# Down-projection of an 8-chunk FFN group: gating at the exit from PSUM, accumulation into DRAM by DMA, and another order for an inner tile's differences

## The chip, the cores and the metric

The kernel runs on one core of one Trainium2 chip. The metric is device time in microseconds (us); 3 runs of the kernel before took 1652.31 to 1652.87, with a median of 1652.55. The core has engines that run side by side, each with its own queue in order: TensorE (PE) multiplies matrices into PSUM, VectorE (DVE) and ScalarE (ACT) do elementwise work and can read PSUM, GpSimd (POOL) and SyncE (SP) issue DMAs here. A wait in a queue holds everything behind it.

## The reference

One step of a diffusion backbone, one trunk layer, for 128 context and 512 latent tokens of width 1024, in float32:

```python
h = modulate(rmsnorm(x, norm_g[0]), sh1, sc1)
x = x + 0.5 * g1 * swiglu(h, ffn1_w1, ffn1_w2)
h = modulate(rmsnorm(x, norm_g[1]), shm, scm)
y, C, n, m = mixer(h, ...)          # mLSTM both ways, short convolution
x = x + gm * y
h = modulate(rmsnorm(x, norm_g[2]), sh2, sc2)
x = x + 0.5 * g2 * swiglu(h, ffn2_w1, ffn2_w2)
```

where `swiglu(h, w1, w2) = (silu(a) * b) @ w2` and a, b are the halves of `h @ w1`, with an inner width of 2816 = 22 chunks of 128. A final RMSNorm follows. The gate g2 is one vector for context tokens and another for latent tokens. Only the second feed-forward network (FFN) is touched by the change.

## The kernel before, in words

Activations lie transposed: X is 8 tiles of 128 channels by 640 tokens (T), split in halves of 320 (HT): the first half has all 128 context tokens and 192 latent ones, so its gate needs two column ranges, 0 to 128 and 128 to 320; the second half needs one. To keep float32 accuracy, each operand is split into a high part (a cast, ScalarE, line 75) and a low part (a subtraction, VectorE, line 79), and each product is three matmuls (`three`, lines 245 to 247).

Two blocks of weights are multiplied together as a **pair** by a Strassen-like scheme (`pair_steps`): seven products instead of eight, in the order A11, S1, S2, A12, S3, S4, A22, each twelve matmuls of 128x320. Their weights are quarter blocks or sums of them (ws, line 218, VectorE). Their activations are eight lists of four tiles: 11, 21, 22 and the differences T1 to T4; A11 takes 11, S1 takes T1, S2 takes T2, A12 takes 21, S3 takes T3, S4 takes 22, A22 takes T4. Four accumulators in PSUM (a, b, e, c) pass through: b starts as ScalarE's copy of a (line 280), c as its copy of b (line 290); S1's result is copied out as p5 (line 286); after S3, c is read to make c22 = c + p5 (line 301 on VectorE, or with `spare_v` line 298 on ScalarE and 299 on VectorE); only then may A22 go on writing c. After S4, b + p5 (line 304) is handed out. `ev(mi, h, src)` takes the result for block mi and token half h. The results of block 1 are handed out late, at the A11 step of the next pair (`flush`).

At each product the kernel first emits the weight preparation for the product four places ahead (sum, cast, low part), then the matmuls, then what reads the result. After product number i the list `at[i]` is called: work put there by hand. `lazy` is a list of postponed steps, of which `relax` calls all and `relax_some(n)` n. So the order in which each engine's queue gets its work is the order of these calls; no planner changes it.

The second FFN runs in groups of 8, 8 and 6 chunks. A group of eight (`eights`) has two phases. First come the **gate pairs** j: block a and block b of chunk j; ScalarE takes silu of a (line 1033), VectorE multiplies by b (line 1035), giving sa for both token halves. In chunks 0 to 3 that makes list 11 and T1 (steps `left`, `diff1`); in chunks 4 to 7 the steps `diff2`, `diff3`, `diff4` finish T2, 21, 22 and the raw values of T3 and T4 (`raw3`, `raw2`, lines 1019, 1024, 1028), which lie in X's SBUF tiles since X has been stored to DRAM (`xd`, by `spill_x`). In the first group, chunks 0 and 1 are made by an element ahead of the pairs, which leaves a stock of six postponed steps. Then come four **down pairs** m = 0, 2, 4, 6: two blocks of w2 by the eight lists, whose results are gated and added to X. For that X tiles are loaded from DRAM (`x_back`), updated by `add_x` (line 953: x = ps * gate + x on VectorE, three instructions per block), and stored (`x_away`). T3 and T4 of the network's input, saved in `hd`, are loaded again in the last down pair (`h_back`): eight loads after S3, eight after A22. All these DMAs stand in POOL's queue. The gate's columns are `modT[:, g, m, 0:1]` for latent and `1:2` for context tokens. The six-chunk group at the end uses other code and X in SBUF; `x_whole` loads it.

Of the kernel before, what the change touches and what calls it, by code (L numbers as in the profile page):

```python
# [44 lines left out]
def mixer_step(ctx: ExitStack, tc: tile.TileContext, x_prompt, x_sample, state_C, state_n, state_m,  # L45
# [23 lines left out]
    def t3():  # L69
        return tp.tile([P, HT], F32, name="t3", bufs=8)  # L70
# [171 lines left out]
    def three(ps, hi, lo, kk, act, start, stop):  # L242
        ws = slice(kk * P, (kk + 1) * P)
        ah, al = act
        PE.matmul(ps, hi[:, ws], ah, start=start, stop=False, skip_group_check=True)  # L245
        PE.matmul(ps, hi[:, ws], al, start=False, stop=False, skip_group_check=True)  # L246
        PE.matmul(ps, lo[:, ws], ah, start=False, stop=stop, skip_group_check=True)  # L247
# [15 lines left out]
    def relax_some(n):  # L263
        for _ in range(min(n, len(lazy))):
            lazy.pop(0)()

    def pair_steps(order, ev, spare_v, acts):
        S = {}

        def prod(name, ps, start):  # L270
            hi, lo = op()
            for kk in range(4):
                three(ps[:, :HT], hi, lo, kk, acts[ACT_OF[name]][kk], start and kk == 0, kk == 3)

        for name in order:
            if name == "A11":
                S["a"] = big()
                prod(name, S["a"], True)
                S["b"] = big()
                A.copy(S["b"][:, :HT], S["a"][:, :HT])  # L280
                flush()
            elif name == "S1":
                e = big()
                prod(name, e, True)
                S["p5"] = t3()
                A.copy(S["p5"], e[:, :HT])
            elif name == "S2":
                prod(name, S["b"], False)
                S["c"] = big()
                A.copy(S["c"][:, :HT], S["b"][:, :HT])  # L290
            elif name == "A12":
                prod(name, S["a"], False)
                ev(0, 0, S["a"][:, :HT])
            elif name == "S3":
                prod(name, S["c"], False)
                S["c22"] = t3()
                if spare_v:
                    A.copy(S["c22"], S["c"][:, :HT])
                    V.tensor_add(S["c22"], S["c22"], S["p5"])
                else:  # L300
                    V.tensor_add(S["c22"], S["c"][:, :HT], S["p5"])  # L301
            elif name == "S4":
                prod(name, S["b"], False)
                V.tensor_add(S["p5"], S["b"][:, :HT], S["p5"])
                ev(0, 1, S["p5"])
            else:
                prod(name, S["c"], False)
                late.append(lambda: ev(1, 0, S["c"][:, :HT]))
                late.append(lambda: ev(1, 1, S["c22"]))
            yield  # L310

    def pair_el(load1, load2, ev, e1=None, spare_v=False, acts=HB, at=None, calm=False):
        po = pair_ops(e1=e1)
        at = at or {}

        def emit():
            nf = len(fill)
            for i, _ in enumerate(pair_steps(ORDER, ev, spare_v, acts)):
                if not calm:
                    relax(7 - i if i else 9)  # L320
                drain(nf - nf * (i + 1) // 7)
                for f in at.get(i, ()):
                    f()
        return dict(element([load1, load2], [po[name] for name in ORDER], emit), pair=True)
# [637 lines left out]
            SQ.pop(0)()  # L962


    def x_back(m, x):
        G.dma_start(x, xd[m])

    def x_away(m, x):
        G.dma_start(xd[m], x)

    def h_away(*names):
        for o in names:
# [4 lines left out]
    def h_back(o):  # L977
        for k in range(4):
            HB[o][k] = hpair(o)
            for i in range(2):  # L980
                G.dma_start(HB[o][k][i], hd[o, k, i])

    def eights(w1, w2, g, f0, n_head, head, more, back):

        spare = (n_head, n_head + 1, 7) if f0 < n_head else (7,)
        UB = {o: [None] * 4 for o in OPS_H}

        def tile_of(m):
            if "xs" not in PO:
                PO["xs"] = [xp.tile([P, T], (F32, F32R)[i // 4], name="x", bufs=KT) for i in range(KT)]  # L990
            return PO["xs"][m]
        slot = lambda a, k: tile_of(2 * a + k // 2)[:, hsl(k % 2)]
        raw3 = lambda k: slot(0, k)
        raw2 = lambda k: slot(1, k)

        def put_own(o, k, src):
            UB[o][k] = hl = upair()
            split(src, *hl)

        def put_22(k, src):  # L1000
            UB["22"][k] = hl = [tile_of(4 + k)[:, hsl(i)] for i in range(2)]
            split(src, *hl)

        def put_lent(o, k, src):
            UB[o][k] = hl = hpair(o)
            split(src, *hl)

        def ev_of(j):
            sa, k = {}, j % 4

            def left():
                put_own("11", k, sa[0])

            def diff1():
                V.tensor_sub(raw2(k), raw3(k), sa[0])
                put_own("T1", k, raw2(k))

            def diff2():
                V.tensor_sub(raw2(k), sa[1], raw2(k))
                put_own("T2", k, raw2(k))  # L1020

            def diff3():
                put_own("21", k, sa[0])
                V.tensor_sub(raw3(k), sa[1], raw3(k))

            def diff4():
                put_22(k, sa[1])
                V.tensor_sub(raw2(k), sa[0], raw2(k))

            def ev(mi, h, src):  # L1030
                if mi == 0:
                    sa[h] = raw3(k) if h and j < 4 else t3()
                    A.activation(sa[h], src, AF.Silu)
                    return
                V.tensor_mul(sa[h], src, sa[h])
                if h == 0:
                    if j < 4:
                        lazy.append(left)
                else:
                    lazy.extend([diff1] if j < 4 else [diff2, diff3, diff4])  # L1040
            return ev
        grp = []
        for j in range(8):
            p = (w_load(w1, 0, KT, (f0 + j) * P, 2 * DFF), w_load(w1, 0, KT, DFF + (f0 + j) * P, 2 * DFF), ev_of(j))
            at = {}
            if j == 7:
                lent = lambda k: lambda: put_lent("T3", k, raw3(k))
                at = {4: [lent(0), lent(1), lent(2)], 6: [flush]}
            due = j - n_head if f0 < n_head else 8
            if due:  # L1050
                at[1] = [relax if due > 2 else lambda n=due + 2: relax_some(n)]
            if f0 + j < n_head:
                head.extend(blocks_of(p))
            else:
                grp.append(pair_el(*p, at=joined(at, more.get(j, {})), spare_v=j in spare, calm=True))
        w2s = []
        away = lambda *ms: [lambda m=m: x_away(m, tile_of(m % 4)) for m in ms]
        come = lambda *ms: [lambda m=m: x_back(m, tile_of(m % 4)) for m in ms]
        PO["x_end"] = away(6, 7)
        for m in range(0, KT, 2):  # L1060
            ev = lambda mi, h, src, m=m: add_x(m + mi, h, src, g, False, tile_of((m + mi) % 4))
            at = {}
            if m == 0:
                four = lambda k: lambda: put_lent("T4", k, raw2(k))
                at = {0: [relax], 1: [lambda: put_lent("T3", 3, raw3(3))] + come(0, 1) + [four(0)],
                      2: [four(1)], 3: [four(2), four(3)] + come(2, 3)}
            else:
                at = {1: away(m - 2, m - 1)}
                if m + 2 < KT:
                    at[2] = come(m + 2, m + 3)  # L1070
                else:
                    at[4] = [lambda: h_back("T3")] if back else []
                    at[6] = [lambda: h_back("T4")] if back else []
            w2s.append(pair_el(w_load(w2, f0 * P, 8, m * P, D), w_load(w2, f0 * P, 8, (m + 1) * P, D), ev,
                               spare_v=True, acts=UB, at=at))
        return grp, w2s

    def ffn(w1, w2, g, lists, head_of, n_head, e1=None, groups=(6, 6, 6, 4), more={}):
# [1051 lines left out]
    def x_whole():  # L2130
        for m in range(KT):
            x_in(m)
    x_end = [lambda: [f() for f in PO["x_end"]]]
    x_in_last = {1: x_end, 2: [x_whole]}
    more = {0: {3: {0: [lambda: h_away("T3", "T4")]}},
            1: {0: {1: x_end}}, 2: {0: x_in_last}}
    head, els = ffn(ffn2_w1, ffn2_w2, G2, y_after, lambda bl: head_el(bl, *right_chain(2, SH2), mod_mid(G2, 0)), 2,
                    groups=(8, 8, 6), more=more)
    els[0][0][0]["fill"] = [step(f) for f in N["later"] + [lambda: None] * 6]
# [37 lines left out]
```

## Time and profile before

| | |
|---|---|
| runs, median (range) | 1652.55 us (1652.31 to 1652.87) |
| profiled execution | 1651.78 us, its span 1649.9 us |
| granted TensorE clock | 0.999 |
| busy: PE, PEld (weight loads), DVE, ACT, POOL | 1628.9, 1585.9, 1319.5, 826.4, 223.3 us |
| first group: gate pairs, down pairs | about 1240 to 1319, 1319 to 1368 us |
| second group: gate pairs, down pairs | about 1368 to 1467, 1467 to 1518 us |
| X tiles: loads and stores of 320 KB from POOL | 32 and 32, 4.0 and 5.4 us from issue to landing |

A timeline row has the start in us from the span's start, the duration, the engine, the line, the operation, output and inputs with their shapes, and in brackets the idle time just ahead and what ended it. A row of a group has the count, the total in us and the mean in ns. A row of windows has the stretch, its length, and the busy time with the number of instructions for PE, PEld, DVE, ACT and POOL, then the clock, the DMA share and GB/s. Matmuls overlap each other: they start about 0.15 us apart and take 0.31.

### The profile page before, as it was taken

How to read it: one execution, taken by the hardware profiler on the slowest of the kernel's cores; microseconds unless marked ns; L12 is line 12 of the kernel's file. 1: busy time of each engine (PE TensorE's matmuls, PEld its weight loads, DVE VectorE, ACT ScalarE, POOL GpSimd, SP SyncE). 2: the span in 40 equal slices, each digit the busy share in tenths (PEclk: the TensorE clock that was granted, in tenths of full speed). 3: DMA queues.
4: the chain of work that ended last, by engine and by line, in shares of the span. 5: the costliest groups of instructions: out<-in, count | busy, mean ns of one | idle time of the engine just before them, and what ended most of it. 6: DMA issues, size and time to landing. Idle time of an engine off the chain costs nothing.

```text
span 1649.9 us, 29478 instructions
## 1 busy us (share of the span) xinstructions
PE 1628.9 (99%) x11093; PEld 1585.9 (96%) x11093; DVE 1319.5 (80%) x2786; ACT 826.4 (50%) x1805; POOL 223.3 (14%) x354
## 2 busy tenths in 40 slices
PE   8999999999999999999999999999999999999998
PEld 5999999999999999999999999999999999999997
DVE  6867887887778878788897899779688897898765
ACT  5642542542566655465561455633275555564443
POOL 2010000000031321221121221011112012003002
PEclk9999999999999999999999999999999999999999
DMA  9454343343353433342258432357355256337522
GB/s 321 116 165 120 105 128 112 103 125 94 114 172 102 102 101 90 84 118 71 84 180 263 113 90 78 106 169 222 117 166 141 84 178 175 88 117 219 172 81 64
DMA packets 283661, 216.68 MB, mean 131 GB/s; under 512 B 9331, under 2 KB 260602, under 8 KB 283520
## 3 DMA queue, kind: packets, MB, share of 16 engines
q1 hardware_dynamic: 263152, 158.36, 33.4%
q0 software_dynamic: 20336, 56.45, 11.5%
q8 instruction: 87, 1.43, 0.4%
q14 instruction: 54, 0.44, 0.1%
q10 hardware_dynamic: 32, 0.01, 0.0%
HBM read 188.98 MB, written 25.79 MB: 130 GB/s over the span
## 4 chain that ended last, share of the span: by engine, by line
PE 89%; DVE 4%; ACT 3%; DMA 2%; issue 1%; POOL 0%; SPq 0%; ACTq 0%; DVEq 0%
PE ps L245 27%; PE ps L246 27%; PE ps L247 27%; PE ax L1717 2%; PE ax L1748 2%; PE ax L1720 1%; DVE wl L79 1%; ACT wh L75 1%; ACT Uh L867 1%; DMA early<-in_w_mod_dram 1%; DMA HT4l<-hd 1%; PE ax L1694 1%; DMA wr<-in_ffn_w_dram 0%; ACT Uh L75 0%; DVE Uh L859 0%
## 5 line engine op out<-in xcount | busy, mean ns | idle before, releaser
L79 DVE TENSOR_TENSOR wl<-wr,wh 128x512 fp32r<-128x512 f32 (+1 forms) x389 | 261.4, 684 | 79.8 <-ACT wh L75 77.5
L75 ACT CAST wh<-wr 128x512 fp32r<-128x512 f32 (+1 forms) x391 | 230.2, 600 | 89.1 <-PE ps L246 69.3
L79 DVE TENSOR_TENSOR wl<-ws,wh 128x512 fp32r<-128x512 f32 x324 | 228.0, 704 | 39.5 <-ACT wh L75 38.7
L75 ACT CAST wh<-ws 128x512 fp32r<-128x512 f32 x324 | 199.0, 620 | 108.9 <-DVE ws L218 71.4
L245 PE MATMUL ps<-Uh,wh 128*128 128x320 f32 x576 | 179.8, 312 | 0.0
L246 PE MATMUL ps<-Ul,wh 128*128 128x320 f32 x576 | 177.9, 309 | 0.2
L247 PE MATMUL ps<-Uh,wl 128*128 128x320 f32 x576 | 177.7, 309 | 0.0
L245 PE MATMUL ps<-HT4h,wh 128*128 128x320 f32 x408 | 128.5, 315 | 0.2 <-DVE t L301 0.2
L246 PE MATMUL ps<-HT4l,wh 128*128 128x320 f32 x408 | 126.3, 309 | 0.5 <-DMA HT4l<-hd 0.4
L247 PE MATMUL ps<-HT4h,wl 128*128 128x320 f32 x408 | 126.0, 309 | 0.0
L245 PE MATMUL ps<-H11h,wh 128*128 128x320 f32 x376 | 118.8, 316 | 0.7 <-ACT H11h L75 0.7
L245 PE MATMUL ps<-H21h,wh 128*128 128x320 f32 x376 | 117.7, 313 | 0.0
L246 PE MATMUL ps<-H11l,wh 128*128 128x320 f32 x376 | 116.5, 310 | 0.3
L247 PE MATMUL ps<-H21h,wl 128*128 128x320 f32 x376 | 116.2, 309 | 0.0
L247 PE MATMUL ps<-H11h,wl 128*128 128x320 f32 x376 | 116.1, 309 | 0.0
L246 PE MATMUL ps<-H21l,wh 128*128 128x320 f32 x376 | 116.0, 308 | 0.0
L245 PE MATMUL ps<-HT3h,wh 128*128 128x320 f32 x356 | 112.0, 315 | 3.5 <-ACT ps L290 3.5
L246 PE MATMUL ps<-HT3l,wh 128*128 128x320 f32 x356 | 110.0, 309 | 0.0
L247 PE MATMUL ps<-HT3h,wl 128*128 128x320 f32 x356 | 110.0, 309 | 0.0
L245 PEld LDWEIGHTS ps<-Uh,wh 128*128 128x128 f32 x576 | 108.1, 188 | 1.4 <-issue 0.8
L246 PEld LDWEIGHTS ps<-Ul,wh 128*128 128x128 f32 x576 | 108.1, 188 | 0.7 <-DVE Ul L79 0.7
L247 PEld LDWEIGHTS ps<-Uh,wl 128*128 128x128 f32 x576 | 108.1, 188 | 0.0
(477 smaller groups left out, 4699.4 us busy)
## 6 DMA issues: line engine op xcount, KB each, us to landing
wr<-in_ffn_w_dram SPq DMA_DIRECT2D x102, 512.0 KB, 3.9
wr<-in_w_in_dram SPq DMA_DIRECT2D x72, 512.0 KB, 3.9
wr<-in_w_mod_dram SPq DMA_DIRECT2D x51, 512.0 KB, 3.9
wr<-in_ffn_w_dram SPq DMA_DIRECT2D x32, 384.0 KB, 3.3
xd<-x POOLq DMA_DIRECT2D x32, 320.0 KB, 5.4
x<-xd POOLq DMA_DIRECT2D x32, 320.0 KB, 4.0
early<-in_w_mod_dram SPq DMA_DIRECT2D x13, 512.0 KB, 9.0
mg<-in_w_mod_dram POOLq DMA_DIRECT2D x8, 512.0 KB, 5.6
```

The costliest lines, as they stand in the source:

```text
L75: A.copy(hi, raw)
L79: V.tensor_sub(lo, raw, f32(hi))
L245: PE.matmul(ps, hi[:, ws], ah, start=start, stop=False, skip_group_check=True)
L246: PE.matmul(ps, hi[:, ws], al, start=False, stop=False, skip_group_check=True)
L247: PE.matmul(ps, lo[:, ws], ah, start=False, stop=stop, skip_group_check=True)
L867: A.activation(t[:, a:b], t[:, a:b], AF.Identity, scale=sc_, bias=bi_)
L1694: PE.matmul(p[:, :P], S["k", dt][:, sl], S["q", dt][:, sl], start=(dt == 0), stop=(dt == 1))
L1717: PE.matmul(p2[:, :DH + 1], S["q", dt][:, sl], S["C"][d][:, dt, :], start=(dt == 0), stop=(dt == 1))
L1720: PE.matmul(p1[:, :DH + 1], S["p", ch][:, d, :], PO["vt"][:, ch, :], start=True, stop=True)
L1748: PE.matmul(p[:, :DH + 1], kw[:, dt * P:(dt + 1) * P], PO["vt"][:, ch, :], start=True, stop=True)
```

## The change

In the groups of eight, X no longer comes back for the down pairs. A result is gated on its way out of PSUM into a free SBUF tile y, and a DMA with accumulation adds y to X in DRAM.

- S1's result is taken out twice by ScalarE, multiplied by the latent gate of block 0 and of block 1 (the second token half has latent tokens only).
- After S3 and after S4, one VectorE instruction makes gate * accumulator + gated p5 straight from PSUM, into the second half of y. This replaces lines 298, 299 and 304 there.
- The first half of y is made by two ScalarE activations (Copy with the gate as scale), for 128 and 192 tokens.
- `x_add` issues one accumulating DMA per block from POOL; `x_back` and `x_away` are gone, and `x_end` with them.
- `x_whole` (the six-chunk group) moves from its gate pair 0 to pair 2.
- The steps of an inner tile are reordered: list 21 is now made in `diff2`, 22 in `diff3`, and T2 with the last subtraction in `diff4`. In the gate pairs two postponed steps are called after S1, and after A12 two more (first group, pairs 3 and 4) or all the rest; before, all were called after S1 (three and four in pairs 3 and 4).

```diff
-    def pair_steps(order, ev, spare_v, acts):
+    def pair_steps(order, ev, spare_v, acts, gated=None):
...
+        def gated_sum(i, ps):
+            y, g = gated(i)
+            V.scalar_tensor_tensor(y[:, HT:], ps[:, :HT], g, S["p5"][i], op0=OP.mult, op1=OP.add)
...
-                S["p5"] = t3()
-                A.copy(S["p5"], e[:, :HT])
+                if gated:
+                    S["p5"] = [t3(), t3()]
+                    for i in range(2):
+                        A.activation(S["p5"][i], e[:, :HT], AF.Copy, scale=gated(i)[1])
...
+                if gated:
+                    gated_sum(1, S["c"])
...
+                if gated:
+                    gated_sum(0, S["b"])
+                    ev(0, 1, None)
...
-    def x_back(m, x):
-        G.dma_start(x, xd[m])
-
-    def x_away(m, x):
-        G.dma_start(xd[m], x)
+    def x_add(m, y):
+        G.dma_start(xd[m], y, accum_op=OP.add)
...
             def diff2():
                 V.tensor_sub(raw2(k), sa[1], raw2(k))
+                put_own("21", k, sa[0])
+
+            def diff3():
+                V.tensor_sub(raw3(k), sa[1], raw3(k))
+                put_22(k, sa[1])
+
+            def diff4():
                 put_own("T2", k, raw2(k))
-
-            def diff3():
-                put_own("21", k, sa[0])
-                V.tensor_sub(raw3(k), sa[1], raw3(k))
-
-            def diff4():
-                put_22(k, sa[1])
                 V.tensor_sub(raw2(k), sa[0], raw2(k))
...
-                at[1] = [relax if due > 2 else lambda n=due + 2: relax_some(n)]
+                at = joined(at, {1: [lambda: relax_some(2)], 3: [lambda: relax_some(2)] if due < 3 else [relax]})
...
+            rows_ = lambda i, m=m: (tile_of((m + i) % 4), modT[:, g, m + i, 0:1])
+
+            def ev(mi, h, src, m=m):
+                y = tile_of((m + mi) % 4)
+                if h:
+                    x_add(m + mi, y)
+                    return
+                for a, b, cd in ((0, P, 1), (P, HT, 0)):
+                    A.activation(y[:, a:b], src[:, a:b], AF.Copy, scale=modT[:, g, m + mi, cd:cd + 1])
...
-    more = {0: {3: {0: [lambda: h_away("T3", "T4")]}},
-            1: {0: {1: x_end}}, 2: {0: x_in_last}}
+    more = {0: {3: {0: [lambda: h_away("T3", "T4")]}}, 2: {2: {1: [x_whole]}}}
```

More of the change, by code (lines that the diff above doesn't have):

```diff
@@ L284, in pair_steps @@
                 prod(name, e, True)
-                S["p5"] = t3()
-                A.copy(S["p5"], e[:, :HT])
+                if gated:
+                    S["p5"] = [t3(), t3()]
+                    for i in range(2):
+                        A.activation(S["p5"][i], e[:, :HT], AF.Copy, scale=gated(i)[1])
+                else:
+                    S["p5"] = t3()
+                    A.copy(S["p5"], e[:, :HT])
             elif name == "S2":
@@ L295, in pair_steps @@
                 prod(name, S["c"], False)
-                S["c22"] = t3()
-                if spare_v:
+                S["c22"] = None if gated else t3()
+                if gated:
+                    gated_sum(1, S["c"])
+                elif spare_v:
                     A.copy(S["c22"], S["c"][:, :HT])
@@ L303, in pair_steps @@
                 prod(name, S["b"], False)
-                V.tensor_add(S["p5"], S["b"][:, :HT], S["p5"])
-                ev(0, 1, S["p5"])
+                if gated:
+                    gated_sum(0, S["b"])
+                    ev(0, 1, None)
+                else:
+                    V.tensor_add(S["p5"], S["b"][:, :HT], S["p5"])
+                    ev(0, 1, S["p5"])
             else:
@@ L310, in pair_steps, with pair_el @@
             yield
-    def pair_el(load1, load2, ev, e1=None, spare_v=False, acts=HB, at=None, calm=False):
+    def pair_el(load1, load2, ev, e1=None, spare_v=False, acts=HB, at=None, calm=False, gated=None):
         po = pair_ops(e1=e1)
@@ L317, in emit @@
             nf = len(fill)
-            for i, _ in enumerate(pair_steps(ORDER, ev, spare_v, acts)):
+            for i, _ in enumerate(pair_steps(ORDER, ev, spare_v, acts, gated)):
                 if not calm:
@@ L1056, in eights @@
         w2s = []
-        away = lambda *ms: [lambda m=m: x_away(m, tile_of(m % 4)) for m in ms]
-        come = lambda *ms: [lambda m=m: x_back(m, tile_of(m % 4)) for m in ms]
-        PO["x_end"] = away(6, 7)
         for m in range(0, KT, 2):
-            ev = lambda mi, h, src, m=m: add_x(m + mi, h, src, g, False, tile_of((m + mi) % 4))
+            rows_ = lambda i, m=m: (tile_of((m + i) % 4), modT[:, g, m + i, 0:1])
[6 more added lines that the diff above has]
+                    A.activation(y[:, a:b], src[:, a:b], AF.Copy, scale=modT[:, g, m + mi, cd:cd + 1])
             at = {}
@@ L1064, in eights @@
                 four = lambda k: lambda: put_lent("T4", k, raw2(k))
[L1065 to L1073, printed above, removed]
+                at = {0: [relax], 1: [lambda: put_lent("T3", 3, raw3(3)), four(0)], 2: [four(1)], 3: [four(2), four(3)]}
+            elif m == KT - 2 and back:
+                at = {4: [lambda: h_back("T3")], 6: [lambda: h_back("T4")]}
             w2s.append(pair_el(w_load(w2, f0 * P, 8, m * P, D), w_load(w2, f0 * P, 8, (m + 1) * P, D), ev,
-                               spare_v=True, acts=UB, at=at))
+                               acts=UB, at=at, gated=rows_))
         return grp, w2s
@@ L2132, in x_whole @@
             x_in(m)
-    x_end = [lambda: [f() for f in PO["x_end"]]]
-    x_in_last = {1: x_end, 2: [x_whole]}
-    more = {0: {3: {0: [lambda: h_away("T3", "T4")]}},
-            1: {0: {1: x_end}}, 2: {0: x_in_last}}
+    more = {0: {3: {0: [lambda: h_away("T3", "T4")]}}, 2: {2: {1: [x_whole]}}}
     head, els = ffn(ffn2_w1, ffn2_w2, G2, y_after, lambda bl: head_el(bl, *right_chain(2, SH2), mod_mid(G2, 0)), 2,
```

## The prediction

> **What bounds the kernel now.** I read the page first, then the waits of TensorE, then the timeline around each place where TensorE paused.
>
> ```profile
> span 1649.9 us, 29478 instructions
> PE 1628.9 (99%) x11093; PEld 1585.9 (96%) x11093; DVE 1319.5 (80%) x2786; ACT 826.4 (50%) x1805; POOL 223.3 (14%) x354
> ...
> PE ps L245 <- ACT ps L290: 3.5, 4, 2.2
> ...
> PE ps L246 <- DMA HT4l<-hd: 0.4, 1, 0.4
> ...
> PE ps L245 <- DVE t L301: 0.2, 1, 0.2
> ```
>
> TensorE is busy 99% of the span and the change leaves its 11093 matmuls alone. So time can come only from pauses of TensorE, and in the stages that change there are few: waits for ScalarE's copy at L290, one for a DMA, one for VectorE. The timeline of TensorE gives each (a bracket is the idle time that it shows).
>
> ```profile
> 1285.70 0.31 PE L247 MATMUL ps<-H21h,wl 128*128 128x320 f32 x1
> 1288.24 0.41 PE L245 MATMUL ps<-HT3h,wh 128*128 128x320 f32 x1 [2.22 <-ACT ps L290]
> 1288.49 0.31 PE L246 MATMUL ps<-HT3l,wh 128*128 128x320 f32 x1
> ...
> 1273.42 0.42 PE L245 MATMUL ps<-HT3h,wh 128*128 128x320 f32 x1 [0.75 <-ACT ps L290]
> 1292.22 0.41 PE L245 MATMUL ps<-HT4h,wh 128*128 128x320 f32 x1 [0.20 <-DVE t L301]
> 1326.63 0.41 PE L245 MATMUL ps<-HT3h,wh 128*128 128x320 f32 x1 [0.27 <-ACT ps L290]
> 1475.32 0.41 PE L245 MATMUL ps<-HT3h,wh 128*128 128x320 f32 x1 [0.28 <-ACT ps L290]
> 1530.28 0.42 PE L246 MATMUL ps<-HT4l,wh 128*128 128x320 f32 x1 [0.39 <-DMA HT4l<-hd]
> ...
> 1323.53 0.38 PE L245 MATMUL ps<-Uh,wh 128*128 128x320 f32 x1
> 1324.03 0.42 PE L246 MATMUL ps<-Ul,wh 128*128 128x320 f32 x1
> 1472.31 0.31 PE L245 MATMUL ps<-Uh,wh 128*128 128x320 f32 x1
> 1472.72 0.42 PE L246 MATMUL ps<-Ul,wh 128*128 128x320 f32 x1
> ...
> 1340.00:1350.00 10.00, 10.00 (x71) 10.00 (x70) 8.68 (x17) 4.11 (x9) 2.17 (x4) 1.00 0.74 237
> ```
>
> The last row is a full window: 71 matmuls touch its 10 us, each 0.31 long, so (10 + 0.31) / 71, with rounding 0.147 us, is the step from one to the next: 1.76 us a product of twelve, 12.3 us a pair of seven. 1285.70 to 1288.24 and on to 1288.49 is 2.54 + 0.25 us for two steps: 2.49 lost, the bracket plus 0.27. By the same rule the others lose 1.02, 0.47, 0.54, 0.55 and 0.66 us. The pauses inside a product (0.50 and 0.41 us between matmuls, plus about 0.1 of refill) lose 0.46 and 0.36. Together 6.6 us: 4.0 in the first group's gate pairs, 1.0 and 0.9 in the two first down pairs, 0.7 at the last. That is the most the change can win where it acts. The window shows the opposite too: at 1340 to 1350, inside the down pairs, TensorE is full (10.00 of 10.00), so VectorE time taken from there buys nothing by itself.
>
> **VectorE's work removed.** The down pairs' groups, from 1318.5 to 1368:
>
> ```profile
> L953 DVE SCALAR_TENSOR_TENSOR x<-t,modT,x 128x320 f32<-128x320 f32 x7 | 3.8, 547 | 0.1
> L953 DVE SCALAR_TENSOR_TENSOR x<-ps,modT,x 128x192 f32<-128x192 f32 x7 | 2.8, 407 | 0.0
> L304 DVE TENSOR_TENSOR t<-ps,t 128x320 f32<-128x320 f32 x5 | 2.4, 489 | 0.2
> L953 DVE SCALAR_TENSOR_TENSOR x<-ps,modT,x 128x128 f32<-128x128 f32 x7 | 2.4, 346 | 0.2
> L299 DVE TENSOR_TENSOR t<-t,t 128x320 f32<-128x320 f32 x4 | 2.0, 489 | 0.8 <-ACT t L298 0.7
> ...
> L298 ACT COPY t<-ps 128x320 f32<-128x320 f32 x4 | 1.7, 424 | 5.4 <-PE ps L247 5.4
> ```
>
> Per pair go L299, L304 and six L953: 0.49 + 0.49 + 2 x (0.35 + 0.41 + 0.55) = 3.6 us; two gated sums come, 0.55 each by the L953 row from SBUF (0.49 if they cost what L304 does): 2.5 us less, 20 us over eight pairs. ScalarE loses L298 and gains one 320-wide and four shorter gated copies. The trace of these stages shows none; by L298 they cost up to 0.42 each, 1.7 us more a pair; were each twice that, 3.8 more would still fit into 12.3 us on an engine that was busy 4.11 of 10 in the window above. In pairs two to four all this lies beside full TensorE: 0. If that cover went, a late read of c would cost TensorE directly, see below.
>
> **The cost in the same edit.** In S3, ScalarE's copy of c is replaced by VectorE's gated sum, and A22 may not write c until that is read. VectorE is in order. In the first down pair it is far behind:
>
> ```profile
> 1322.47 0.48 DVE L1019 TENSOR_TENSOR x<-t,x 128x320 f32<-128x320 f32 x1
> 1323.48 0.49 DVE L79 TENSOR_TENSOR Ul<-x,Uh 128x320 fp32r<-128x320 f32 x1 [0.53 <-ACT Uh L75]
> ...
> 1325.10 0.48 DVE L1028 TENSOR_TENSOR x<-t,x 128x320 f32<-128x320 f32 x1
> 1325.50 0.68 DVE L79 TENSOR_TENSOR wl<-ws,wh 128x512 fp32r<-128x512 f32 x1
> ...
> 1331.71 0.48 DVE L299 TENSOR_TENSOR t<-t,t 128x320 f32<-128x320 f32 x1
> ```
>
> Starts follow each other by 0.40 us (320 wide) and 0.60 us (512). T2's low half, today right after its difference, moves behind the low half of 21, L1024 and that of 22: it starts at 1322.47 + 4 x 0.40 = 24.07 instead of 23.48, 0.6 us later, with the 0.53 bubble gone. TensorE waits for it already today. In gate pair 7 the last difference, now after A12, waits for ScalarE, which first waits for A12: a new bubble like the 0.53, which delays the chain of VectorE by about 0.45. So the T2 pause grows by 1.05; the L290 pause (0.54) vanishes behind it: +0.5 at S3. From T2's low half to the gated sum lie, besides itself, six 320-wide and six 512-wide instructions: 0.40 + 2.4 + 3.6 = 6.4, end at 6.95. A22 is due 0.49 + 0.45 + three products = 6.2 after the same point. A22 waits 0.8, with refill +0.9. Each group's first down pair is thus 1.4 us worse. Bounds: 0 (VectorE there in time) to 1.9 (nothing of L290 won).
>
> The rows put the read of a 320-wide c at 424 ns on ScalarE and 489 to 547 on VectorE. [...]
>
> **The order of the differences.** Gate pairs 4 and 5 of the first group owe four and six steps after S1; now two come there and the rest after A12.
>
> ```profile
> 1282.53 0.43 ACT L286 COPY t<-ps 128x320 f32<-128x320 f32 x1 [0.76 <-PE ps L247]
> ...
> 1287.77 0.41 ACT L290 COPY ps<-ps 128x320 f32<-128x320 f32 x1
> ...
> 1288.27 0.48 DVE L1028 TENSOR_TENSOR x<-t,x 128x320 f32<-128x320 f32 x1
> 1291.69 0.48 DVE L301 TENSOR_TENSOR t<-ps,t 128x320 f32<-128x320 f32 x1
> ```
>
> In pair 5, ScalarE has two casts and one weight cast ahead of L290 instead of six and one: it starts about 2.8 us after L286's start and ends at 3.2, and S3 is due at 3.3. S3 no longer waits. But VectorE then has, counted from L286's start: cast and low half of 11 1.25, L1015 0.52, cast and low half of T1 0.9, three 512-wide 1.8 (4.5 with latencies), six steps after A12 2.4, two 512-wide 1.2, so L301 runs from 8.2 to 8.65. A22 is due at 6.84 (four products, less the 0.2 by which L286 starts after S2 has): the stall moves from S3 to A22, 1.9 us, against 2.49 + 0.47. In pair 4 the three VectorE steps and a bubble take 1.8 instead of 2.4: 1.3 us with refill 1.4, against 1.02, and it hands VectorE 0.5 us late to pair 5. Net, both pairs: A22 of pair 5 starts near 1291.6 instead of 1292.22, and pair 6 gives back 0.1: 0.5 us won, of 4.0. The second group's pairs 5 and 6 get the bubble too: 0.1 each, +0.2. Bounds: 4.0 won (L301 in time) to 1 lost.
>
> **DMAs and POOL's queue.**
>
> ```profile
> xd<-x POOLq DMA_DIRECT2D x32, 320.0 KB, 5.4
> x<-xd POOLq DMA_DIRECT2D x32, 320.0 KB, 4.0
> ...
> 1372.92 0.56 POOL L981 DMA_DIRECT2D HT4l<-hd  x1
> ...
> DMA to landing us min/median/max: 3.8/6.3/6.6
> ...
> DMA to landing us min/median/max: 4.2/6.9/9.0
> ```
>
> Sixteen loads and sixteen stores become sixteen accumulates. None is in the trace; bounds are one store (5.4) and store plus load (9.4). A tile is written again about 19 us after its add is issued: 0 either way. Moved: the six-chunk group's X loads go 25 us later, past the HT4 loads. These landed in up to 6.6 us at the first group's end and 9.0 at the second's (the two landing rows), where the 0.66 pause is; it goes: -0.7. The add of block 6 now stands between the HT3 and HT4 loads. Its data are ready some 3 us after S3, the HT3 issues take eight times 0.53 = 4.2, so it costs HT4 one issue, 0.55. The first group's last HT4 lands by 1372.9 + 6.6 = 1379.5; its matmul ran at 1381.03, so 1.5 us of slack remain to pay from: 0.
>
> ```profile
> 1381.03 0.31 PE L246 MATMUL ps<-HT4l,wh 128*128 128x320 f32 x1
> ```
>
> **Sum.** -0.5 (first gate pairs) + 1.4 + 0.2 + 1.4 (down pairs, second gate pairs) - 0.7 = +1.8 us on the profiled execution's 1651.78 (span 1649.9 and 1.9 around it). The median of the runs is 0.77 above that execution: 1652.55 + 1.8 = **1654.3 us**.
>
> **Rivals.** *VectorE keeps up* (faster): the reads of c come in time, since some bubbles I count do not arise. For it: before, L301 held TensorE once only, 0.20. Against: from L1028 at 1288.27 to L301 at 1291.69 are 3.42 us, L1028's own 0.40 and five weight instructions of 0.60, so VectorE had no gap to win. The A22 waits of 1.4, 1.9, 0.9, 0.9 and 0.2 go: 1654.3 - 5.3 = 1649.0. *HT4 comes late* (slower): the accumulate ahead of HT4 reads and writes DRAM on the same 16 DMA engines; if HT4 lands after more than about 7.5 us at both ends, as the 9.0 row shows it can, TensorE waits 1.5 at the first, and 1.3 at the second against the forecast (0.7 not won, 0.6 by the added issue): 1657.1. Against: the X loads that stood beside it then are gone. *It does not do what it says*: the relief is hidden, the reordering only swaps one wait for another, only the DMA moves tell: 1651.8.
>
> **Numbers.** Forecast 0.5, its own range 1651 to 1657; VectorE keeps up 0.25; HT4 late 0.15; nothing 0.1. About 0.2%, 3.3 us, is what a measurement can tell from no change. Faster 0.25; slower 0.25 (HT4 late and the upper end of the forecast); same 0.5. The range goes down past the first rival to 1647.5, up to 1658.
>
> **What would show it.** Right: no wait for L290 over 0.3 us in the gate pairs, but waits of A22 for L301 of 1 us or more in pairs 4 and 5; waits of A22 for the gated sum in the first down pair of each group only; T2's low half as the longest pause there; no HT4 wait. Wrong: A22 without waits (then faster), ScalarE waiting for an accumulate before it writes a tile, or HT4 waits at both ends.

## The result, and the profile after

The changed kernel took 1658.43 us, the median of six runs (1656.78 to 1661.2); the kernel before, run beside it, 1652.43 (1651.03 to 1653.06). The ratio is 1.0039, with a 95% interval of 1.0026 to 1.0052: the change made the kernel slower by 6.0 us. The forecast was 1654.3, its range ended at 1658.0.

The page of the changed kernel's profiled execution (1661.2 us, the longest of the six) has these rows: the span, the busy time of the engines, POOL's DMA queue.

```profile
span 1659.4 us, 29424 instructions
PE 1634.8 (99%) x11093; PEld 1589.0 (96%) x11093; DVE 1303.1 (79%) x2738; ACT 835.8 (50%) x1837; POOL 218.9 (13%) x338
...
q0 software_dynamic: 20080, 51.20, 11.6%
```

VectorE lost 16 us of work and POOL 16 instructions, and the end came later: neither sets it. The waits of TensorE tell more (us in all, times, longest):

```profile
PE ps L245 <- DVE t L312: 3.0, 2, 1.8
PE ps L245 <- DVE x L277: 1.5, 2, 0.8
...
PE ps L246 <- DMA HT4l<-hd: 1.5, 5, 0.4
PE ps L246 <- DVE Ul L79: 1.4, 2, 0.7
...
PE ps L245 <- ACT Uh L75: 0.6, 2, 0.3
...
PE ps L245 <- DMA HT4h<-hd: 0.2, 1, 0.2
```

Line 312 is the old 301 (VectorE reads c in the gate pairs), 277 the gated sum, 299 the old 290. The 2.22 us wait for the copy of c in the gate pairs is gone, as is every other wait for it. In its place stand VectorE's reads of c, T2 (Uh, Ul), and HT4. TensorE's timeline gives the places:

```profile
1277.85 0.42 PE L245 MATMUL ps<-HT4h,wh 128*128 128x320 f32 x1 [1.12 <-DVE t L312]
1292.28 0.42 PE L245 MATMUL ps<-HT4h,wh 128*128 128x320 f32 x1 [1.84 <-DVE t L312]
1325.93 0.41 PE L245 MATMUL ps<-Uh,wh 128*128 128x320 f32 x1 [0.35 <-ACT Uh L75]
1327.05 0.42 PE L246 MATMUL ps<-Ul,wh 128*128 128x320 f32 x1 [0.71 <-DVE Ul L79]
1333.66 0.42 PE L245 MATMUL ps<-HT4h,wh 128*128 128x320 f32 x1 [0.76 <-DVE x L277]
1384.36 0.41 PE L246 MATMUL ps<-HT4l,wh 128*128 128x320 f32 x1 [0.33 <-DMA HT4l<-hd]
1385.83 0.41 PE L246 MATMUL ps<-HT4l,wh 128*128 128x320 f32 x1 [0.35 <-DMA HT4l<-hd]
...
1538.23 0.41 PE L246 MATMUL ps<-HT4l,wh 128*128 128x320 f32 x1 [0.24 <-DMA HT4l<-hd]
1539.69 0.41 PE L246 MATMUL ps<-HT4l,wh 128*128 128x320 f32 x1 [0.30 <-DMA HT4l<-hd]
```

I count a loss as in the prediction: from one start to the next, less the step of 0.147. All losses at a place together:

| us lost by TensorE | before | after | difference | forecast |
|---|---|---|---|---|
| first group, gate pairs 4 to 6 | 3.98 | 3.76 | -0.2 | -0.5 |
| second group, gate pairs | 0 | 0.55 | +0.55 | +0.2 |
| first down pair, first group | 1.00 | 2.61 | +1.6 | +1.4 |
| first down pair, second group | 0.91 | 2.53 | +1.6 | +1.4 |
| HT4 at both groups' ends | 0.66 | 4.23 | +3.6 | -0.7 |
| sum | 6.6 | 13.7 | +7.1 | +1.8 |

Four rows came as forecast, within 0.35 us each. One did not, and it is the largest. The other 2.3 of the 9.4 us between the two profiled executions go with the clock: in these three windows of this one TensorE ran below full clock (the column after POOL's), where the kernel before had 1.00. They hold two stretches, the first of them across two windows. The first made the work behind it only 0.5 us later (one matmul ahead of the gate pairs starts at 1215.94 before and at 1216.42 here); the second stands where TensorE is full, and cost 10 x (1 - 0.83) = 1.7.

```profile
24.00:32.00 8.00, 6.50 (x55) 4.86 (x56) 4.21 (x14) 0.62 (x1) 0.00 (x0) 0.90 1.09 360
32.00:40.00 8.00, 8.00 (x58) 5.22 (x60) 5.04 (x14) 4.00 (x10) 0.00 (x0) 0.88 1.12 334
1290.00:1300.00 10.00, 8.16 (x46) 7.90 (x45) 7.57 (x15) 3.66 (x8) 0.00 (x0) 0.83 0.18 54
```

### The profile page after: what moved, and what is told of

The parts are those of the page before. It is cut to its first block, busy times and chain, and to the rows that moved or that the text cites. A ratio compares the mean times of both kernels' runs of the same rounds, so it can differ in the third digit from the quotient of the medians.

```text
span 1659.4 us, 29424 instructions
## 1 busy us (share of the span) xinstructions
PE 1634.8 (99%) x11093; PEld 1589.0 (96%) x11093; DVE 1303.1 (79%) x2738; ACT 835.8 (50%) x1837; POOL 218.9 (13%) x338
## 3 DMA queue, kind: packets, MB, share of 16 engines
q0 software_dynamic: 20080, 51.20, 11.6%
## 4 chain that ended last, share of the span: by engine, by line
PE 88%; DVE 4%; ACT 3%; DMA 2%; issue 1%; SPq 1%; POOL 0%; ACTq 0%; DVEq 0%
PE ps L245 27%; PE ps L246 27%; PE ps L247 27%; PE ax L1728 2%; PE ax L1759 2%; PE ax L1731 1%; DVE wl L79 1%; DMA HT4l<-hd 1%; DMA xd<-x 1%; DMA wr<-in_ffn_w_dram 1%; PE ax L1705 1%; ACT Uh L882 1%; ACT wh L75 0%; PE ax L600 0%; DVE ws L218 0%
```

## The experiments

Every kernel was run beside the kernel before, on the same chip; as that moved a little (1651.8 to 1652.4), I give the difference from it too. A comparison's 95% interval reaches about 1.5 to 2 us to each side, and the losses of TensorE come from one profiled execution each. Several of the kernels share these edits: *c by ScalarE* means that ScalarE copies c out of PSUM and VectorE reads the copy; *split order* is the change's calls of the postponed steps after S1 and after A12.

### The HT4 loads

First, only the place of block 6's add in POOL's queue.

```diff
-                    x_add(m + mi, y)
+                    if m + mi != KT - 2:
+                        x_add(m + mi, y)
...
-    at = {4: [lambda: h_back("T3")], 6: [lambda: h_back("T4")]}
+    at = {4: [lambda: h_back("T3")], 6: [lambda: h_back("T4"), lambda: x_add(KT - 2, tile_of((KT - 2) % 4))]}
```

> The changed kernel, but the add of block 6 is issued after the HT4 loads instead of between the HT3 and the HT4 loads. Theory A (the add of block 6 holds up the HT4 loads in POOL's queue and in the DMA engines behind it): the HT4 waits of TensorE at both groups' ends, 2.6 and 1.6 us in the profile of the changed kernel, go or fall below 0.5 each, and the time falls by 3 to 4 us to about 1654.5. Rival B (accumulating DMAs slow all transfers, wherever they stand): the HT4 waits stay above 1 us each and the time stays above 1657.

Measured: 1656.47 us, 4.4 above before, so 1.5 below the change, half of what was expected. The losses at HT4 shrank to 0.4 at one end and none at the other, as expected. Then the kind of DMA: block 6 alone, and all sixteen, as plain stores at the same places.

```diff
-        G.dma_start(xd[m], y, accum_op=OP.add)
+        G.dma_start(xd[m], y)
```

> The changed kernel, but block 6 of each group is stored to X in DRAM by a plain DMA at the same place in the queue, not accumulated. So X's block 6 loses what was in it before: the sum with X is left out there, and nothing else. If it is the accumulation itself that makes HT4 late (0.86 us of POOL for its issue against 0.55, and a read and a write of X on the DMA engines), a good part of the HT4 waits (2.65 and 1.58 us in the profile) goes: 1656.9 us. If the place ahead of the HT4 loads alone does it, the time stays at 1658.4.

> The changed kernel with all sixteen accumulating DMAs replaced by plain stores to X in DRAM: what is left out is the sum with the X that was there. Queue order, number and place of the DMAs are those of the change. If reading and adding in DRAM on the DMA engines is what delays HT4, its waits go and their spread with them: 1658.4 - 2.0 = 1656.4 us or a little below, runs within 2 us. If the place ahead of the HT4 loads does it, the time stays within 0.7 us of 1658.4 with runs over 4 us apart. One block alone stored plainly gave 1657.1, between the two.

Measured: 1657.08 and 1657.42 us, both 5.2 above before; the second lies between its two expectations, and its runs are 2.8 us apart. The losses at HT4 went from 4.2 to 2.1 with one store and to 0.6 with sixteen. POOL's timeline at the first group's end, the change first, then all stores:

```profile
1369.68 0.55 POOL L993 DMA_DIRECT2D HT3l<-hd  x1 [1.02 <-issue]
...
1373.42 0.53 POOL L993 DMA_DIRECT2D HT3h<-hd  x1 [1.02 <-PE ps L247]
...
1374.46 0.94 POOL L981 DMA_DIRECT2D xd<-x  x1
1375.02 0.92 POOL L993 DMA_DIRECT2D HT4h<-hd  x1
...
1377.11 0.95 POOL L993 DMA_DIRECT2D HT4h<-hd  x1
1379.32 0.53 POOL L993 DMA_DIRECT2D HT4l<-hd  x1 [1.25 <-DMA HT3h<-hd]
1380.64 0.53 POOL L993 DMA_DIRECT2D HT4h<-hd  x1 [0.79 <-DMA HT3l<-hd]
1381.97 0.53 POOL L993 DMA_DIRECT2D HT4l<-hd  x1 [0.80 <-DMA xd<-x]
```

```profile
1373.74 0.53 POOL L993 DMA_DIRECT2D HT3h<-hd  x1 [2.16 <-PE ps L247]
...
1374.78 0.57 POOL L981 DMA_DIRECT2D xd<-x  x1
...
1377.39 0.60 POOL L993 DMA_DIRECT2D HT4h<-hd  x1
1378.79 0.53 POOL L993 DMA_DIRECT2D HT4l<-hd  x1 [0.80 <-DMA HT3h<-hd]
1379.43 0.53 POOL L993 DMA_DIRECT2D HT4h<-hd  x1
1380.03 0.53 POOL L993 DMA_DIRECT2D HT4l<-hd  x1
```

The last three HT4 issues wait until earlier DMAs of the same queue have landed, 2.84 us with accumulation and 0.80 without; the DMA that a bracket names is each time the eighth before in the queue. The accumulate's own place in the queue costs little: the next issue starts 0.56 us after it. The DMA view from 1350 to 1392 (packets, MB, share of 16 engines; KB each and median landing), again the change first:

```profile
q0 software_dynamic: 3116, 4.46, 54.0%
...
xd<-x POOLq DMA_DIRECT2D x5, 320.0 KB, 4.9
...
HT4h<-hd POOLq DMA_DIRECT2D x4, 160.0 KB, 7.3
```

```profile
q0 software_dynamic: 2704, 4.26, 34.6%
...
xd<-x POOLq DMA_DIRECT2D x5, 320.0 KB, 3.4
...
HT4h<-hd POOLq DMA_DIRECT2D x4, 160.0 KB, 4.8
```

So accumulation makes HT4 later than the same DMAs as stores: its loads land later, and later issues wait for those landings. It is not the whole delay. Counted from S3's first matmul of the last down pair (at 1363.75 before, 1367.19 in the change, 1367.49 with all stores), the first HT4 load is issued 5.09 us later in the kernel before and 7.83 in both others, and the last 9.17, 14.78 and 12.54 later. So 2.2 of the 5.6 us by which the last issue moved come with accumulation, and 3.4 come with plain stores too. In that part the HT3 loads alone make 2.2: at the first group's end the change, the kernels with the add moved and with one store, and below the accumulating kernel with T2's step alone have two waits of 1.01 to 1.03 among them, all stores has one of 2.16, and the kernel before none. What they wait for stays open: the first bracket names nothing and the second TensorE, whose products with T3 were done by then.

The medians fell by less than the profiles' losses, 0.8 us with all stores and 1.5 with the add moved, for 4 us; neither is clear of the intervals. Two runs with all stores took 1654.9 and 1655.5 (mean clock 0.999), five 1656.8 to 1657.7 (0.997 to 0.998); the profiled one is the longest of these and holds a stretch of lower clock (0.81 from 1288 to 1296), so some of what HT4 gave back may have gone there. Three kernels below leave HT4 and block 6's add as in the change, and their profiles lose 2.0 us there (the old order), 3.2 (c by ScalarE in the down pairs) and 4.0 (c by ScalarE in the gate pairs); in the kernels below with accumulation and the add behind HT4 it is 0.5 at most. So the waits and their removal are shown, but their size varies from execution to execution, and how much of the change's median is theirs stays open.

The moved X loads, alone in the kernel before:

> The kernel before with one part of the change alone: the X loads of the six-chunk group go from its gate pair 0 to pair 2, past the HT4 loads of the second group's end. If these loads caused the 0.66 us pause for HT4 there, it goes: 1652.4 - 0.7 = 1651.7 us. If they only collide elsewhere, the time is 1652.4 or more. A difference of 0.7 is near what the runs can tell; the pause in the profile decides.

Measured: 1652.55 us against 1652.24, ratio 0.9999 (0.9990 to 1.0008). The profile shows no wait for HT4, so the loads had caused it; its 0.66 us are too little for the runs, and this profile too had a stretch at low clock, from 1289 (0.79 over 1288 to 1296).

### VectorE's queue

The old order of the differences under the new down-projection, and the new order alone in the kernel before:

> The changed down-projection with the differences and the postponed steps in the order of before. Theory A (the new order only swaps waits): S3 of gate pairs 4 and 5 waits for L290 again, about 4.0 us in all instead of 3.8 for A22 plus 0.6 in the second group; in the first down pairs the T2 pause falls from 1.5 to about 0.5 but S3 waits about 0.9 and A22 about 1.2: the time stays within 1 us of 1658.4. Rival B (the new order is what costs): about 1654.

> The kernel before with the new order of the differences and postponed steps alone; the down pairs load, update and store X as before. Theory A: the waits of the gate pairs change from 4.0 to 4.4 (first group 3.8, second 0.6), the first down pairs lose about 1.5 each at T2 instead of 1.0 for T2 and L290: 1653.9, between +1 and +2. Rival B (the order is the main cost): +4 or more, 1656.5 and up.

Measured: 1659.14 us (7.1 above before) and 1654.35 (2.3 above). Beside the old down-projection the new order loses; in the change it seems to win about 1.1, which is less than these two comparisons can differ by. In the first, the waits for the copy of c were back (4.5 us in four places: 0.7 and 2.2 in the gate pairs, 0.8 in each first down pair); in the second, the gate pairs' A22 waits for VectorE were those of the change.

```profile
PE ps L245 <- ACT ps L299: 4.5, 4, 2.2
```

Next, c by ScalarE: in the down pairs, then in all gate pairs.

```diff
-                    gated_sum(1, S["c"])
+                    y, g = gated(1)
+                    S["c22"] = t3()
+                    A.activation(S["c22"], S["c"][:, :HT], AF.Copy, scale=g)
+                    V.tensor_add(y[:, HT:], S["c22"], S["p5"][1])
```

> The changed kernel, but after S3 ScalarE copies c times the gate to SBUF and VectorE adds the gated p5 from there, so A22 waits for ScalarE alone. Theory A (A22 of each first down pair waits for VectorE, which is behind): the two waits of 1.0 us go, time 2 us lower, about 1656.4. Rival B (TensorE then meets the same backlog one step later, at the next wait of the pair): no gain, 1658.4.

```diff
-        spare = (n_head, n_head + 1, 7) if f0 < n_head else (7,)
+        spare = range(8)
```

> The changed kernel, but in all gate pairs ScalarE copies c out of PSUM and VectorE adds p5 from SBUF (lines 308 to 310) instead of VectorE reading c (line 312). The order of the postponed steps stays. If the waits of A22 in gate pairs 4 to 6 come only from VectorE's arrears (1.39, 2.10, 0.27 in the first group, 0.55 in the second), they go: 1658.4 - 4.3 = 1654.1 us. If the stretch at half clock that followed the 2.1 us pause in two profiles is tied to that pause, it goes too and the runs lie closer together than the 4.4 us of the changed kernel. Rival: VectorE's arrears only move on, to the weights or to S3 of the next pair; then 1656.5 or more.

Measured: 1657.03 us (5.0 above before) and 1653.99 (2.1 above). A22's waits for VectorE were gone in the profiles, from the first down pairs in the one and from the gate pairs in the other, and no new wait stood in their place. The second time is as expected (1654.1): it is the one edit to the change whose gain, 3.9 us, is clear of the intervals. The first gained 1.0 of the 2.0 expected, which the runs cannot tell from nothing; there the profile decides.

### Everything at once, with and without accumulation

Four edits in both kernels: c by ScalarE, split order, steps of gate pair 7 called after its last product, T3's last and T4's first tiles split only after ScalarE's copy of c (line 290). With accumulation also block 6's add behind HT4; without, the X loads moved as above.

```diff
-                at = {4: [lent(0), lent(1), lent(2)], 6: [flush]}
+                at = {4: [lent(0), lent(1), lent(2)], 6: [flush, relax]}
...
-  at = {0: [relax], 1: [lambda: put_lent("T3", 3, raw3(3)), four(0)], 2: [four(1)], 3: [four(2), four(3)]}
+  at = {0: [relax], 2: [lambda: put_lent("T3", 3, raw3(3)), four(0), four(1)], 3: [four(2), four(3)]}
```

> The kernel before, no accumulation, with four edits: postponed steps split between S1 and A12 as in the change, but their old order; ScalarE copies c out in all gate pairs; the steps of gate pair 7 are called right after its last product, and the casts of T3 (last tile) and T4 (first tile) in the first down pair come after ScalarE's copy at line 290; the X loads of the six-chunk group go to its pair 2. If each pause of TensorE is only the wait of one engine's queue as I read it, 4.0 us of the gate pairs, 1.9 of the two first down pairs and 0.7 of HT4 go: 1652.4 - 6.6 = 1645.8 us. Rival: VectorE's arrears come out at other places; then about half is won, 1649.

> The changed kernel with accumulation kept and its new waits taken away: add of block 6 issued after the HT4 loads, ScalarE reads c in the down pairs and in all gate pairs, the steps of gate pair 7 called right after its last product, casts of T3 (last tile) and T4 (first tile) after line 290. If the 13.7 us that TensorE lost in the profile of the changed kernel are all such queue waits, 4.3 (A22 in gate pairs), 1.8 (A22 in first down pairs), 2 (HT4, by the earlier run) and 3.1 (T2) go: about 1647 us; if the T2 pauses stay, 1650. If accumulation costs something beyond these waits, it stays above the same edits without accumulation.

Measured: 1653.3 us without accumulation (ratio 1.0009) and 1650.52 with it (0.9992, 0.9984 to 1.0001). The plain kernel came out 7.5 us above its expectation (1645.8), the other 0.5 above the upper end of its own (1647 to 1650). In the plain kernel X's first tiles are loaded while the last raw values of T3 still lie there, so T3 is computed in part from X. In both, the waits of A22 for VectorE and the 2.2 us wait for the copy of c were gone from the gate pairs (1.4 us of smaller pauses stayed in the plain kernel), and a new pause stood in each first down pair: S2 waited for ScalarE's copy of a (line 280, in the accumulating kernel 284), 2.3 and 2.1 us, 1.6 and 1.5. I had put casts ahead of that copy which wait for VectorE. The next two kernels call only T2's step there, T2 first; the plain one also loads X's second tile later and has the change's order of the differences in the other pairs:

```diff
-                at = {4: [lent(0), lent(1), lent(2)], 6: [flush, relax]}
+                at = {4: [lent(0), lent(1), lent(2)], 6: [flush, lambda: relax_some(1)]}
```

> The same schedule without accumulation: X tiles loaded, updated, stored as before; postponed steps and T2 of gate pair 7 as in the kernel with accumulation; c read by ScalarE; X loads of the six-chunk group later; the first X tiles loaded only once T3's raw values there are read. If the hand order is what was won and the accumulation brings nothing by itself: 1652.4 - 6.6 = 1645.8 us, at or below the same order with accumulation. If the 20 us of VectorE time that accumulation saves matter in the down pairs, or the plain loads and stores hold something up, it is above it by 1 us or more.

> The last kernel with accumulation (1650.5 us), whose two largest pauses, 1.59 and 1.51 us, are ScalarE's copy of a at line 284 standing behind the casts that I had put after gate pair 7. Here only the first step of that pair, the difference for T2 and its cast, comes there, T2 first as in the kernel before; the other two come after the copy. If the queue order is all, both pauses go: 1650.5 - 3.1 = 1647.4 us. If T2's low half is late again as in the change (0.4 to 1.5 us each), 1648.3 to 1650.5.

Measured: 1648.81 us (0.9982, 0.9973 to 0.9991) and 1649.78 (0.9985, 0.9976 to 0.9994). Both are faster than the kernel before, and both still lost 1.5 to 1.6 us at each S2, against the forecast. Then T2's step was taken ahead of A22, since it needs only the half that is ready after S4:

```diff
+                if early:
+                    ev(1, 1, S["c22"])
...
-                at = {4: [lent(0), lent(1), lent(2)], 6: [flush, lambda: relax_some(1)]}
+                at = {4: [lent(0), lent(1), lent(2)], 5: [lambda: relax_some(1)], 6: [flush]}
```

> The plain kernel with the better order (1648.8 us), whose two largest pauses, 1.58 and 1.51 us, are S2 of the first down pair waiting for ScalarE's copy of a (line 280), which stood behind the cast for T2, which waited for VectorE. In gate pair 7 the second half of block 1, which needs no A22, is now multiplied right after S4, and T2's difference and cast are called there. If these pauses are queue order alone, they go: 1648.8 - 3.1 = 1645.7 us. If VectorE's arrears, then about 2 us, decide, half or less is won: 1647.3 or more.

> The same edit on the accumulating kernel with the better order (1649.8 us; pauses of 1.60 and 1.52 us at line 284): 1646.7 us if queue order alone sets them, 1648.3 or more if half or less is won. It tells too whether accumulation still costs about 1 us beside the plain order, as the last pair of runs had it.

Measured: 1648.8 us and 1648.79; the pauses shrank by 0.2 to 0.3 us only. That the step's place alone set them is refuted. The timeline of VectorE and ScalarE in the plain kernel shows what did (the last matmul of S1 starts at 1317.91):

```profile
1316.69 0.46 ACT L75 CAST Uh<-x 128x320 fp32r<-128x320 f32 x1 [1.08 <-DVE x L1034]
1317.06 0.62 ACT L75 CAST wh<-wr 128x512 fp32r<-128x512 f32 x1
1317.18 0.49 DVE L79 TENSOR_TENSOR Ul<-x,Uh 128x320 fp32r<-128x320 f32 x1 [0.53 <-ACT Uh L75]
1317.59 0.68 DVE L218 TENSOR_TENSOR ws<-wr 128x512 f32<-128x512 f32 x1
...
1318.39 0.62 ACT L75 CAST wh<-ws 128x512 fp32r<-128x512 f32 x1 [0.71 <-DVE ws L218]
...
1318.91 0.42 ACT L280 COPY ps<-ps 128x320 f32<-128x320 f32 x1
```

T2 (Uh, Ul) is in time now. The copy stands behind a weight cast, the cast waits for a weight sum, and the sum stands in VectorE's queue: VectorE's arrears, the work that it is late with, reach TensorE through another instruction. So I took work away from ahead of that place, the low parts of T3 and T4:

```diff
-                at = {4: [lent(0), lent(1), lent(2)], 5: [lambda: relax_some(1)], 6: [flush]}
+                at = {5: [lambda: relax_some(1)], 6: [flush]}
...
-  at = {0: [relax], 2: [lambda: put_lent("T3", 3, raw3(3)), four(0), four(1)], 3: [four(2), four(3)]}
+  at = {0: [relax], 1: [lent(0), lent(1), lent(2)], 2: [lent(3)], 3: [four(k) for k in range(4)]}
```

> The plain kernel of 1648.8 us with one more edit: the first three T3 tiles are split (cast and low part) after S1 of the first down pair instead of after S3 of gate pair 7, and all of T4 after A12. In the profile ScalarE's copy of a (line 280) stands behind a weight cast that waits for VectorE's sum (line 218), and VectorE is late there, by the 1.29 us of the T3 low parts and by two bubbles of 0.54. If those low parts are the arrears, the S2 pauses of 1.32 and 1.35 us shrink to 0.2 or less: 1648.8 - 2.3 = 1646.5 us. Rival: the arrears come out a product or two later, at line 290 or at S3 (T3 late): 1648 or more.

> The same edit on the accumulating kernel of 1648.8 us: 1646.5 us if the T3 low parts are the arrears, 1648 or more if they come out later. VectorE has 2.5 us less to do per down pair here, so that it should make up its arrears at least as soon as the plain kernel; if accumulation has a use in this schedule, it shows as the lower of the two.

Measured: 1651.75 us without accumulation (0.9998, 0.9989 to 1.0007) and **1648.1** with it (0.9978, 0.9968 to 0.9987), the lowest time here. S2's pauses fell to 0.13 us in both (0.23 with refill), so the arrears were behind them. In the plain kernel they came out later and larger, at low parts of T4 and T3, as the rival had it: 5.6 us lost in the two first down pairs, 3.6 before this edit. In the accumulating one they came out later too, in small pieces: 2.3 against 2.9. Waits of TensorE, plain first:

```profile
PE ps L246 <- DVE HT4l L79: 1.6, 2, 0.9
...
PE ps L246 <- DVE HT3l L79: 0.4, 2, 0.2
```

```profile
PE ps L245 <- ACT ps L299: 0.7, 2, 0.4
```

All losses from 1215 to 1570 are 7.9 us in the one profile and 4.7 in the other, a difference of 3.2 for 3.65 in the medians. In this order the accumulating kernel is more than 3 us faster, and the waits that it lacks are for VectorE or for ScalarE's copies. That the VectorE time which accumulation saves is what decides is likely, not tested by itself. Nor is accumulation ahead as such: in the order before this edit both kernels took 1648.8, and against the best plain kernel (3.4 below before) the best accumulating one (3.9 below) is not clear of the intervals.

### A pause put back

```diff
-        spare = range(8)
+        spare = [j for j in range(8) if f0 or j != 5]
```

> The plain kernel with that edit, and one pause put back: in gate pair 5 of the first group VectorE reads c again, as in the change, so A22 waits there for about 2 us. By the wait alone: 1.9 to 2.1 us above the same kernel without it, and the mean clock of its runs as there. If a pause of this length also brings a stretch at half clock in part of the executions (1.7 us each time), it is 1.9 to 3.8 us above, with runs further apart than 2.1 us and some of them at a mean clock of 0.997.

Measured: 1651.57 us, 2.8 above the same kernel without the pause; the pause itself, up to 1292.69, lost 2.1 in the profile. Eight runs lie between 1651.14 and 1651.77, three between 1653.43 and 1654.16. The profiled execution is one of the three, but its stretch at low clock is not behind the pause; three rows of its windows:

```profile
32.00:40.00 8.00, 8.00 (x46) 5.05 (x45) 5.38 (x17) 3.02 (x7) 0.00 (x0) 0.79 1.12 343
...
1288.00:1296.00 8.00, 6.06 (x41) 5.80 (x40) 7.52 (x16) 3.58 (x8) 0.00 (x0) 1.00 0.24 68
1296.00:1304.00 8.00, 8.00 (x57) 8.00 (x56) 6.93 (x14) 5.29 (x12) 0.00 (x0) 1.00 0.44 131
```

So this run does not show that the pause brings such a stretch.

## Why the prediction was wrong, point by point

- **Where the time could come from** held for the pauses of TensorE, 7.1 of the 9.4 us in the profiles. For the clock, the other 2.3, the prediction had no term. Its step of 0.147 us is right by the rows; the quotient that it gives for it is 0.145.
- **VectorE's work removed, worth nothing by itself**: right for this change, which won nothing by it. The size was 16 us, not 20: VectorE's instructions overlap (they start 0.40 us apart and take 0.48), and the sum added their durations. The gated sum took 548 ns, like the L953 row from which it was priced (547). That VectorE's time buys nothing by itself may be too strong as a general sentence: with the order of the last experiment the accumulating kernel was 3.65 us faster.
- **The cost in the same edit**: T2 pauses and A22's wait for the gated sum, +1.4 per group forecast, +1.6 in the profile. The profile of the run with c on ScalarE confirms the A22 part. The T2 part was right in size; its cause, VectorE's arrears, is argued from its queue. The test by taking work away was made on the pause that stood there in later kernels, not on this one.
- **The order of the differences**: A22 waits of 1.4 and 1.9 forecast, 1.39 and 2.10 in the profile; -0.3 forecast in all, +0.35. The waits were right to 0.2 us each.
- **DMAs and POOL's queue**: the step that failed. It priced the add of block 6 at "one issue, 0.55", to be paid out of 1.5 us of slack, with -0.7 for the X loads: a gain of 0.7, against a loss of 3.6 in the profile. The X part held, and so did the 0.55: the next issue starts 0.56 us after the accumulate. Put at nothing was what follows: HT4 loads behind the accumulate that take 7.3 us to land, not 4.8 (medians, change and all stores), 2.84 us in which POOL stood still between HT4 loads until earlier DMAs had landed, and 2.0 us of waits among the HT3 loads. The loads were counted from issue to landing as if no issue would have to wait. Rows of the kernel before show such waits already, on the X loads behind HT4 at the second end:

```profile
1526.04 0.54 POOL L2009 DMA_DIRECT2D x<-xd  x1 [1.38 <-DMA HT4l<-hd]
...
1529.62 0.54 POOL L2009 DMA_DIRECT2D x<-xd  x1 [1.57 <-DMA HT4h<-hd]
```

- **The rival "HT4 comes late"** named the accumulate ahead of HT4 as the cause, and 1657.1 us, with a chance of 0.15. It is what happened in the profile, with larger waits than its 1.5 and 1.3 (2.65 and 1.58), and HT4 waits at both ends were the prediction's own sign of being wrong. But its condition, loads that land after more than 7.5 us, is only half of it: the last HT4 load landed 5.1 us after its issue, which came 5.6 us late. The argument against it, that the X loads are gone, was true only of the second end.
- **The range** ended where this rival and the forecast's own terms were taken one at a time. By the profile's waits, four terms each 0.2 to 0.35 too low and the rival together give 1652.55 + 7.1 = 1659.65, where 1658.4 was measured; without HT4's waits the medians fell by only 0.8 and 1.5 us, so which part of the 4.2 us between forecast and measurement is HT4's in a typical run stays open.

## What to carry to other kernels

A DMA put ahead of others in one queue is to be priced by what the queue does behind it, the wait of later issues for earlier landings included (2.84 us here), and not by its own issue (0.56); slack of 1.5 us was not cover for that here. When an engine with a queue in order is late, moving one late instruction forward may only change which reader waits (0.2 to 0.3 us won of 1.5 to 1.6); letting another engine do the read won 3.9 us, and taking work from ahead of it gained 0.9 us in one kernel, less than the runs can tell, and cost 2.7 in the other. Two kernels can be equal in one order and 3.65 us apart in the next: compare each in its own best order, where these two differ by less than the runs can tell.

## What the runs showed of the hardware

- An accumulating DMA of 320 KB against a plain store of the same size and place: POOL's issue 0.86 us against 0.55; landing 4.9 against 3.4 us in the rows above. Over the whole kernel the queue took 11.6% of 16 engines' 1659.4 us with accumulates and 10.3% of 1655.9 with stores: an estimate of 22 us of engine time more for each of the sixteen. (In the stretch from 1350 to 1392 the same working, for five, gives 26.) The queue's packets were 20080 against 19056, 64 more for each accumulate. The queue's row on the page of the kernel with all stores:

```profile
q0 software_dynamic: 19056, 51.20, 10.3%
```

- In the profiles of the kernel before and of the change, with 243 and 227 DMAs in POOL's queue, none starts while more than seven earlier ones have not landed; the three HT4 loads of the change that wait for landings, above, start 0.28, 0.51 and 0.28 us after the eighth before each has landed. Whether the chip or the program sets the eight is not shown.
- Stretches of about 3.4 us at half clock inside a stage in which TensorE is otherwise full. In the change the clock was 0.50 from 1293.4 to 1296.8, 1.00 in the microsecond before and 0.99 in the 1.2 us after. In the kernel with the new order alone, one began a microsecond after the pause of A22 in gate pair 5 (windows of 2 us, the clock after POOL's column):

```profile
1292.00:1294.00 2.00, 1.90 (x11) 1.90 (x12) 1.65 (x4) 0.92 (x3) 0.00 (x0) 0.83 0.00 0
1294.00:1296.00 2.00, 2.00 (x9) 2.00 (x9) 1.91 (x4) 0.58 (x2) 0.00 (x0) 0.50 0.00 0
1296.00:1298.00 2.00, 2.00 (x14) 2.00 (x13) 0.79 (x2) 0.49 (x2) 0.00 (x0) 0.82 0.66 199
```

Such a stretch costs some 1.7 us: the three rows lack 0.34, 1.00 and 0.36 us of full clock. It stands there in four of the ten profiles that have a pause of 1.8 us or more in this pair, and in none of the nine that have none; the pause put back had none behind it. That the two belong together is suggested by these counts, not shown; two profiles also have one far from it, the change (0.50 from 30.5 to 33.9 us) and the pause put back (0.79 over 32 to 40).
